# A hybrid block on one core: streamed projection weights prepared in the first stage, and the first gate folded into the output weight

## The chip, the cores and the metric

The kernel runs on one core of one Trainium2 chip. The metric is the device time of one execution in microseconds. Engines are named as in the profile: PE is TensorE (PEld its weight loads), DVE VectorE, ACT ScalarE, POOL GpSimd, SP SyncE, whose queue issues the DMAs. PE's clock is given as the granted clock, 1.00 being 2.4 GHz and 0.50 being 1.2 GHz.

## The reference

One layer over 2048 latent tokens and 256 context tokens of width 1024. `modulate` takes a shift and a scale from a matrix product with `mod_w`; one input projection feeds three mixers (gated linear attention, RWKV-7, retention), whose outputs are concatenated, projected, gated and added; a squared-ReLU MLP follows.

```python
def trunk_layer(xl, xc, c, c_ctx, p, rows, ctx_out):
    ml = jnp.split((jax.nn.silu(c) @ p["mod_w"] + p["mod_b"])[:, None, :], 6, axis=-1)
    ...
    zl = modulate(rms_norm(xl, p["norm1_g"]), ml[0], ml[1]) @ p["w_in"]
    zc = modulate(rms_norm(xc, p["norm1_g"]), mc[0], mc[1]) @ p["w_in"]
    ...
    xl = xl + ml[2] * (jnp.concatenate([yl_gla, yl_rwkv, yl_ret], axis=-1) @ p["w_out"])
    hl = modulate(rms_norm(xl, p["norm2_g"]), ml[3], ml[4])
    xl = xl + ml[5] * squared_relu_mlp(hl, p["mlp_w1"], p["mlp_w2"])
```

The output is a last RMS norm of the latent tokens. `ml[2]` is the first gate (g1 in the kernel).

## The kernel before

**Stages.** The first stage computes the modulation (`modulation1`), the normalised tokens as two float16 halves in SBUF (`h_block`: hT_hi, hT_lo), and the first part of the input projection. The scan then runs the chunks of the RWKV recurrence, the other mixers and the rest of the projection together. `out_proj` is the output projection with the second norm, `mlp` the rest.

**Projection in the first stage.** Columns of `w_in` are taken 128 at a time: L, G, k0, v0, r0, then k1, v1, r1, then k2, v2, r2 and three columns of the gated attention (called ga, gb, gc here). For each, `ip_tile` calls `ip_weights`: load (st), absmax by DVE (L343), the maximum over partitions by POOL (L345), two small DVE operations, a scaled float16 copy wh by ACT (L349) and the remainder wl by DVE (L350). `ip_block` (L390) does one block of 512 tokens, or 256 context tokens, with 24 matmuls (wh with hT_hi, wl with hT_hi, wh with hT_lo, eight each), evicts it on ACT with the scale (L393) and stores it (zc). In the code, the features of head group 0 (`rw_inputs`, `rw_features`: steps of many small operations on all engines, kk at L670 one of them) and `rw_base` (L794, L795) stand between r0 and k1; after r1 come `modulation2` and the first steps of group 1's features, and then k2 to gc. `modulation2` makes the other four rows of the modulation, 32 columns: a load mw, eight DVE operations (L269, L271), and a matmul with ones into one column of the PSUM tile pc (L272), which a second pool with one buffer holds; then mc, pg and the gate row.

**Order.** The instructions of an engine run in a fixed order. The framework sets it when the kernel is built, from the code's order, the priorities and the time at which buffers come free by its own estimate; a tile in a pool of one buffer can't be written before the one that held the buffer has been read. In the scan a planner (`Order`) picks which of its streams (chains of chunks, features, mixers, `ip_stream`) issues next, by estimated PE time; `ip_stream` is added with a count of 363 steps.

**The streamed projection.** `ip_stream` goes through five groups of two or three columns (`STREAM_T`; TV, two gate groups, two of retention), 14 columns in all. For each group it prepares the columns by `ip_weights` into rwh and rwl (one buffer each), then for each of 16 or 18 token tiles loads the stored normalised tokens (rh<-hd), runs 24 matmuls (L1027 is the line of all PE work in the scan), evicts (rzs, L443) and stores z (zt).

**The chains.** Four chunks make a block of the recurrence. Each chunk makes one ACT copy Tsf (L920).

**out_proj.** w_out is split in two float32r parts woh and wol (L1936). Each product pz (L1950) is multiplied by the gate row on DVE (gz, L1954) and added to x on POOL (L1955). Then the second norm: x times its factor (DVE, L1911), plus the shift row b2 (POOL, L1912), and sums of blocks as float16 halves (L1804, L1917, L1918).

Of the kernel before, what the change touches and what calls it, by code (L numbers as in the profile page):

```python
# [11 lines left out]
F32 = mybir.dt.float32  # L12
# [10 lines left out]
P = 128  # L23
# [54 lines left out]
def setup(k):  # L78
    nc, tc, I = k.nc, k.tc, k.I
    cp = k.cpool  # L80
    k.ones_row = cp.tile([1, P], F32, name="ones_row")
    nc.vector.memset(k.ones_row, 1.0)
# [69 lines left out]
def modulation1(k, xp, pp, then):  # L152
# [8 lines left out]
    with tc.tile_pool(name="mo1", bufs=1, side="right") as m1, tc.tile_pool(name="mo2", bufs=1, side="right") as mp:  # L161
# [16 lines left out]
        ones = mp.tile([P, P], F32, name="mones")  # L178
# [73 lines left out]
def modulation2(k, cp, first):  # L252
# [6 lines left out]
    with tc.tile_pool(name="mo2", bufs=2, side="right") as mp, tc.tile_pool(name="mops2", bufs=1, space=PSUM, side="right") as pp:  # L259
        ones = mp.tile([P, 1], F32, tag="ones", name="ones", bufs=1)  # L260
        nc.vector.memset(ones, 1.0)
        pc = pp.tile([P, 4 * KD], F32, tag="pc", name="pc", bufs=1)
# [19 lines left out]
        pt = pp.tile([4 * KD, P], F32, tag="pc", name="pg", bufs=1)  # L282
# [50 lines left out]
def ip_weights(k, wp, wh, wl, srcs, M):  # L333
# [8 lines left out]
    am = wp.tile([P, 1], F32, tag="am", name="am")  # L342
# [11 lines left out]
def ip_tile(k, nm, wp):  # L354
# [4 lines left out]
    return wh, wl, ip_weights(k, wp, wh[:, :, 0:M], wl[:, :, 0:M], srcs, M)  # L359


def ip_channels(k, names, wp, ps, ready=()):

    n = max(len(ready), 1)
    for group in [names[:n]] + [[nm] for nm in names[n:]]:
        tiles = ready if ready and group == names[:n] else [ip_tile(k, nm, wp) for nm in group]
# [5 lines left out]
        for bi in TOK_ORDER:  # L372
            for nm, *t in work:
                ip_block(k, nm, bi, wp, ps, *t)

# [36 lines left out]
def ip_stream(k, wp, ps):  # L412
# [3 lines left out]
    for cols in STREAM_T:  # L416
        W, kind = P * len(cols), cols[0][2]
        wh = wp.tile([P, KD, 384], F16, tag="rwh", name="rwh")
        wl = wp.tile([P, KD, 384], F16, tag="rwl", name="rwl")
        iv = []  # L420
        for u, (src, dst, _) in enumerate(cols):
            cs = slice(P * u, P * u + P)
            ar = ip_weights(k, wp, wh[:, :, cs], wl[:, :, cs], [(0, src, P)], P)
            iv.append(wp.tile([P, 2], F32, tag="iv", name="iv", bufs=6))
            nc.vector.tensor_scalar(iv[u], k.h_inv, ar, 48 ** -0.5 if kind == "v" else 1.0, ALU.mult, ALU.mult)
            yield 4
        yield 6
        for ti in range(2 if kind == "g" else 0, NT):
            n = 256 if ti < 2 and kind == "r" else W
            h = wp.tile([P, 2, KD, P], F16, tag="rh", name="rh", bufs=2)  # L430
# [11 lines left out]
            for u in range(n // P):  # L442
                nc.scalar.activation(zs[:, P * u : P * u + P], pz[:, P * u : P * u + P], AF.Copy, scale=iv[u][:, s : s + 1])  # L443
# [8 lines left out]
        k.streamed += 1  # L452

# [902 lines left out]
def mix_setup(k, mp, ps):  # L1356
# [5 lines left out]
    nc.tensor.matmul(pl, k.ones_row, rate, start=True, stop=True)  # L1362
# [445 lines left out]
def over_partitions(k, ps, pool, x):  # L1808
# [6 lines left out]
    nc.tensor.matmul(pt[:, P : P + 1], k.ones_row, m, start=True, stop=True)  # L1815
# [64 lines left out]
def out_proj(k, es, H, hp):  # L1880
# [6 lines left out]
    with tc.tile_pool(name="opy", bufs=2) as yp, tc.tile_pool(name="opx", bufs=2) as xp, tc.tile_pool(name="opps", bufs=4, space=PSUM) as ps:  # L1887
# [335 lines left out]
```

## Time and profile before

| | |
|---|---|
| timed, median of 3 | 3925.78 us (3912.99 to 3928.82) |
| the profiled execution | 3896.32 us |
| its span | 3894.5 us |
| PE busy | 3370.4 us, 87% |
| DVE busy | 2535.2 us, 65% |
| ACT, POOL busy | 1357.3 us, 35%; 786.4 us, 20% |
| mean granted clock | 0.887 |

The profile gives times from the start of the span. By it, the first stage lasts to about 640 us, the scan to about 2215, out_proj from 2240 to about 2480, and the MLP to the end.

### The profile page before, as it was taken

Reading aid. Unit: us, or ns where it says so; the run is one execution under the profiler, and the core shown is the slowest. Engines: PE = TensorE matmul, PEld = TensorE weight load, DVE = VectorE, ACT = ScalarE, POOL = GpSimd, SP = SyncE. Lnnn points to the kernel's source line nnn. Section 1 sums busy time; section 2 is a strip of 40 time slices with the busy share of each in tenths; the row PEclk is TensorE's granted clock in tenths of the full one; section 3 lists DMA queues with packets and bytes.
Section 4 is the critical chain, followed back from the end, with each engine's and each line's share of the span. In section 5 each row is a group of like instructions: output and inputs, shape, how many; then the busy total and the mean of one; then the engine's idle time right before and its main releaser. Section 6 shows DMA issues by size and latency. Waiting matters only on the chain. (4 is left out here: it accounts for less than half of the span.)

```text
span 3894.5 us, 62894 instructions
## 1 busy us (share of the span) xinstructions
PE 3370.4 (87%) x23493; PEld 2263.0 (58%) x23493; DVE 2535.2 (65%) x5307; ACT 1357.3 (35%) x3033; POOL 786.4 (20%) x940
## 2 busy tenths in 40 slices
PE   7687786699798789899899688888899999999997
PEld 2443445476466567666676566555555566666665
DVE  7555877567585666757567368877777766544446
ACT  3333343334344443525344333333333332221212
POOL 3122335214343122222232235200000001000001
PEclk8898895698788789789898799999999999999998
DMA  7875646345454244343423276653333346322322
GB/s 228 191 210 147 185 143 175 109 137 158 124 165 116 85 113 114 98 102 110 121 88 111 66 211 195 231 186 124 125 128 127 130 123 207 114 90 97 104 87 95
DMA packets 526339, 532.36 MB, mean 137 GB/s; under 512 B 247171, under 2 KB 408710, under 8 KB 525254
## 3 DMA queue, kind: packets, MB, share of 16 engines
q1 hardware_dynamic: 526024, 528.25, 45.6%
q8 instruction: 187, 3.06, 0.3%
q14 instruction: 128, 1.05, 0.1%
HBM read 323.81 MB, written 180.19 MB: 129 GB/s over the span
## 5 line engine op out<-in xcount | busy, mean ns | idle before, releaser
L2005 PE MATMUL pu<-H,wo 128*128 128x512 f16 x2688 | 625.5, 387 | 27.6 <-ACT wo L1841 21.1
L2071 DVE TENSOR_TENSOR acc<-acc,pz 128x512 f32<-128x512 f32 x512 | 348.3, 685 | 373.0 <-PE pz L2069 370.0
L2005 PEld LDWEIGHTS <-wo 128*128 128x128 f16 x2688 | 254.3, 99 | 361.8 <-issue 63.9
L2069 PE MATMUL pz<-w2h,uh 128*128 128x512 f32 x1024 | 439.5, 429 | 27.3 <-ACT uh L2032 25.1
L2069 PE MATMUL pz<-w2l,uh 128*128 128x512 f32 x1024 | 409.7, 400 | 0.0
L2069 PE MATMUL pz<-w2h,ul 128*128 128x512 f32 x1024 | 396.7, 396 | 1.0 <-DVE ul L2034 1.0
L2084 POOL TENSOR_TENSOR acc<-acc,fg 128x1024 f32<-128x1024 f32 x10 | 23.9, 2411 | 1368.7 <-ACT acc L2083 1368.7
L1027 PE MATMUL pz<-rwh,rh 128*128 128x384 f16 (+1 forms) x1376 | 289.0, 340 | 7.7 <-ACT rzs L443 4.8
L1027 PEld LDWEIGHTS <-rh 128*128 128x128 f16 x2064 | 199.5, 105 | 132.5 <-issue 37.9
L2069 PEld LDWEIGHTS pz<-w2h,uh 128*128 128x128 f32 x1024 | 199.0, 194 | 84.4 <-ACT uh L2032 27.4
L2069 PEld LDWEIGHTS pz<-w2l,uh 128*128 128x128 f32 x1024 | 198.8, 194 | 41.2
L2069 PEld LDWEIGHTS pz<-w2h,ul 128*128 128x128 f32 x1024 | 195.4, 191 | 44.6 <-DVE ul L2034 1.4
L390 PEld LDWEIGHTS <-wh 128*128 128x128 f16 (+2 forms) x1072 | 115.8, 111 | 171.9 <-issue 73.1
L2029 ACT ACTIVATE u<-u 128x512 f32<-128x512 f32 x64 | 36.8, 622 | 484.4 <-DVE s L2023 484.4
L390 PE MATMUL pz<-hT_hi,wh 128*128 128x512 f16 (+5 forms) x536 | 133.7, 392 | 61.9 <-ACT zs L393 50.7
L2017 ACT ACTIVATE s<-pu,iv 128x512 f32<-128x512 f32 x96 | 65.5, 685 | 255.9 <-PE pu L2005 255.6
L1027 PE MATMUL pz<-rwl,rh 128*128 128x384 f16 (+1 forms) x688 | 146.0, 344 | 0.7 <-DVE rwl L350 0.7
L1027 PE MATMUL pg<-Z,BK 64*128 64x128 f32 (+1 forms) x864 | 127.3, 320 | 8.4 <-DVE fbon L986 4.9
L1950 PE MATMUL pz<-woh,yh 128*128 128x512 f32 x256 | 104.8, 415 | 26.5 <-DMA x<-in_w_out_dram 16.0
L390 PE MATMUL pz<-hT_lo,wh 128*128 128x512 f16 (+5 forms) x536 | 127.0, 377 | 0.0
L390 PE MATMUL pz<-hT_hi,wl 128*128 128x512 f16 (+5 forms) x536 | 125.2, 374 | 0.0
L1027 PEld LDWEIGHTS pg<-Z,BK 64*128 64x128 f32 x864 | 107.6, 218 | 21.1 <-issue 6.2
(524 smaller groups left out, 7043.0 us busy)
## 6 DMA issues: line engine op xcount, KB each, us to landing
rh<-hd SPq DMA_DIRECT2D x86, 512.0 KB
st<-in_mlp_w_dram SPq DMA_DIRECT2D x64, 512.0 KB
w1d<-wo SPq DMA_DIRECT2D x112, 256.0 KB
wo<-w1d SPq DMA_DIRECT2D x112, 256.0 KB
x<-in_x_dram SPq DMA_DIRECT2D x32, 512.0 KB
mw<-in_mod_w_dram SPq DMA_DIRECT2D x32, 512.0 KB
w2d<-w2h SPq DMA_DIRECT2D x32, 512.0 KB
w2d<-w2l SPq DMA_DIRECT2D x32, 512.0 KB
```

The lines of the kernel that those rows point to most:

```text
L390: nc.tensor.matmul(pz[:M, o : o + step], a[:, kk, 0:M], b[:, kk, t0 + o : t0 + o + step], start=(i == 0), stop=(i == 23))
L1027: return op(out, lhs, rhs, **kw)
L1950: nc.tensor.matmul(pz, a[:, kk], w[:, kk, 512 * hf : 512 * hf + 512], start=(kk + i == 0), stop=(kk == KD - 1 and i == 2))
L2005: nc.tensor.matmul(bank, W[o][:, a, kk], H[o][:, 4 * b + kk], start=(i == 0), stop=(i == 11))
L2017: nc.scalar.activation(s, product(o), AF.Copy, scale=iv)
L2029: nc.scalar.activation(r, r, AF.Relu)
L2069: nc.tensor.matmul(pz, U[q][tb][u][:, ts], W2[q][w][:, cs], start=(i == 0), stop=(i == 5))
L2071: nc.vector.tensor_add(a[:, cs], a[:, cs], pz)
L2084: nc.gpsimd.tensor_mul(a, a, fg)
```

## The change

1. `ip_weights` takes its scale from the sum of squares of the column tile in place of the largest absolute value: ACT squares with an accumulated sum, a matmul with ones (pnrm) adds over partitions, and five small DVE operations make the scale (`norm_scale`). The matmul writes a bank of a new PSUM pool `ipn` with one buffer; modulation2's pc and pg now use that pool and its one buffer too.
2. `ip_channels` prepares the next column ahead of the present one's blocks, and calls `ip_keep` twice after each column behind the first group. `ip_keep` prepares one streamed column and stores both halves to DRAM (wsd), and keeps its scales in SBUF (siv). The 14 calls fall to k1 to ga.
3. `ip_stream` reads a group's weights back with one DMA for each half; the high half of the next group is loaded one token tile ahead. The tag rw has three buffers for both halves. The planner's count is 345.
4. `out_proj` multiplies the rows of w_out by g1 on DVE before they are split; pz is added to x straight on DVE; b2 is added on DVE.
5. The ones tile lives on; two smaller tiles of ones are gone.

```diff
+def norm_scale(k, ps, pool, sq):
+    nc.tensor.matmul(ps, k.ones, sq, start=True, stop=True)
+    x = pool.tile([P, 1], F32, tag="ar", name="ar", bufs=6)
+    nc.vector.tensor_scalar(x, ps, 1e-36, None, ALU.max)
...
+    nc.vector.tensor_scalar(si, x.bitcast(I32), 1, None, ALU.logical_shift_right)
+    nc.vector.tensor_scalar(si, si, -1, 0x5F3759DF, ALU.mult, ALU.add)
+    nc.vector.tensor_scalar(s, s, 0.96 * 2.0 ** 14, None, ALU.mult)
+    nc.vector.reciprocal(x, s)
+    return s, x
...
-    nc.vector.tensor_reduce(am, st[:, :, 0:M], axis=AX.XY, op=ALU.max, apply_absolute_value=True)
-    ar = wp.tile([P, 1], F32, tag="ar", name="ar", bufs=6)
-    nc.gpsimd.partition_all_reduce(ar, am, P, bass_isa.ReduceOp.absmax)
-    nc.vector.tensor_scalar(ar, ar, 1e-30, 2.0 ** -14, ALU.max, ALU.mult)
-    sc = wp.tile([P, 1], F32, tag="sc", name="sc")
-    nc.vector.reciprocal(sc, ar)
+    sq = wp.tile([P, 1], F32, tag="am", name="am")
+    nc.scalar.activation(wh, st[:, :, 0:M], AF.Square, accum_out=sq)
+    sc, ar = norm_scale(k, ps, wp, sq)
     nc.scalar.activation(wh, st[:, :, 0:M], AF.Copy, scale=sc)
     nc.vector.scalar_tensor_tensor(wl, st[:, :, 0:M], sc, wh, ALU.mult, ALU.subtract)
...
+def ip_keep(k, wp):
...
+    g, u = k.keep.pop(0)
+    src, _, kind = STREAM_T[g][u]
+    w = [wp.tile([P, KD, P], F16, tag="w" + x, name="kw" + x, bufs=3) for x in "hl"]
+    ar = ip_weights(k, wp, k.ipn.tile([P, 512], F32, tag="pn", name="pnrm")[:, 0:1], *w, [(0, src, P)], P)
+    k.nc.vector.tensor_scalar(k.siv[:, g, u], k.h_inv, ar, 48 ** -0.5 if kind == "v" else 1.0, ALU.mult, ALU.mult)
+    for d, x in zip(k.wsd[g], w):
+        k.nc.sync.dma_start(d[:, :, P * u : P * u + P], x)
...
     n = max(len(ready), 1)
-    for group in [names[:n]] + [[nm] for nm in names[n:]]:
-        tiles = ready if ready and group == names[:n] else [ip_tile(k, nm, wp) for nm in group]
+    groups = [names[:n]] + [[nm] for nm in names[n:]]
+    tiles = list(ready) or [ip_tile(k, names[0], wp, k.ipn)]
+    for i, group in enumerate(groups):
...
+        ahead = following() if len(group) == 1 else None
...
+        for _ in range(2 if n == 1 else 0):
+            ip_keep(k, wp)
+        tiles = following() if ahead is None else ahead
...
-    with tc.tile_pool(name="mo2", bufs=2, side="right") as mp, tc.tile_pool(name="mops2", bufs=1, space=PSUM, side="right") as pp:
-        ones = mp.tile([P, 1], F32, tag="ones", name="ones", bufs=1)
-        nc.vector.memset(ones, 1.0)
-        pc = pp.tile([P, 4 * KD], F32, tag="pc", name="pc", bufs=1)
+    with tc.tile_pool(name="mo2", bufs=2, side="right") as mp:
+        pp, ones = k.ipn, k.ones[:, 0:1]
+        pc = pp.tile([P, 512], F32, tag="pn", name="pc")[:, 0 : 4 * KD]
...
-        pt = pp.tile([4 * KD, P], F32, tag="pc", name="pg", bufs=1)
+        pt = pp.tile([P, 512], F32, tag="pn", name="pg")[0 : 4 * KD, 0:P]
...
+    def weights(g, i):
+        w = wp.tile([P, KD, 384], F16, tag="rw", name="rw" + "hl"[i], bufs=3)
+        nc.sync.dma_start(w[:, :, 0 : P * len(STREAM_T[g])], k.wsd[g][i])
+        return w
+
+    wh = weights(0, 0)
+    for g, cols in enumerate(STREAM_T):
         W, kind = P * len(cols), cols[0][2]
-        wh = wp.tile([P, KD, 384], F16, tag="rwh", name="rwh")
-        wl = wp.tile([P, KD, 384], F16, tag="rwl", name="rwl")
-        iv = []
-        for u, (src, dst, _) in enumerate(cols):
-            cs = slice(P * u, P * u + P)
-            ar = ip_weights(k, wp, wh[:, :, cs], wl[:, :, cs], [(0, src, P)], P)
-            iv.append(wp.tile([P, 2], F32, tag="iv", name="iv", bufs=6))
-            nc.vector.tensor_scalar(iv[u], k.h_inv, ar, 48 ** -0.5 if kind == "v" else 1.0, ALU.mult, ALU.mult)
-            yield 4
-        yield 6
+        wl = weights(g, 1)
+        if g == 0:
+            yield 8
         for ti in range(2 if kind == "g" else 0, NT):
             n = 256 if ti < 2 and kind == "r" else W
+            if ti == NT - 1:
+                nxt = weights(g + 1, 0) if g + 1 < len(STREAM_T) else None
...
-                nc.gpsimd.tensor_add(x, x, b2)
+                nc.vector.tensor_add(x, x, b2)
...
+            g1 = mod_row(k, xp, 0)
...
+                nc.vector.tensor_mul(st, st, g1)
                 nc.scalar.copy(wh[:, kk], st)
                 nc.vector.tensor_tensor(wl[:, kk], st, wh[:, kk].bitcast(F32), ALU.subtract)
-            with tc.issue_after(load):
-                g1 = mod_row(k, xp, 0)
...
-                        gz = xp.tile([P, 512], F32, tag="gz", name="gz")
-                        nc.vector.tensor_mul(gz, pz, g1[:, cs])
-                        nc.gpsimd.tensor_add(x[:, cs], x[:, cs], gz)
+                        nc.vector.tensor_add(x[:, cs], x[:, cs], pz)
...
+            k.ipn = es.enter_context(tc.tile_pool(name="ipn", bufs=1, space=PSUM, side="right"))
             ip_channels(k, names, wp, ips, ready)
...
-            k.order.add(ip_stream(k, fp, fps), 0, 312, 363, 4)
+            k.order.add(ip_stream(k, fp, fps), 0, 312, 345, 4)
```

**PE in the first stage.** Before, in the midst of the columns k1 to gc, PE's rows are these (L390 the blocks, pc the modulation's columns):

```order
L390 MATMUL pz<-hT_hi,wh 128x256
L272 MATMUL pc<-ones,macc 128x1
L390 LDWEIGHTS wh
L390 MATMUL pz<-hT_hi,wh 128x256
L390 LDWEIGHTS wh
L390 MATMUL pz<-hT_hi,wh 128x256
L390 LDWEIGHTS wh
L390 MATMUL pz<-hT_hi,wh 128x256
L272 MATMUL pc<-ones,macc 128x1
```
The pc matmuls and the features' matmuls lie between the matmuls of the blocks, no more than eight rows of the printed order apart, to the end of the projection. In the changed kernel (L421 is the block, L269 pc, L334 pnrm; pv, pk, pb, px, pu and pn belong to a feature step) PE comes to the end of r1's last block with these rows:

```order
L421 MATMUL pz<-hT_lo,wh 128x512
L421 LDWEIGHTS wh
L421 MATMUL pz<-hT_lo,wh 128x512
L334 MATMUL pnrm<-am,ones 128x1
L682 MATMUL pv<-ident,v 128x128 x3
L334 MATMUL pnrm<-am,ones 128x1
L269 MATMUL pc<-ones,macc 128x1 x2
L784 MATMUL pk<-ident,knw 128x128 x3
L682 MATMUL pv<-ident,E 128x128 x3
L714 MATMUL pb<-s,bones 128x384
L741 MATMUL px<-AR,BK 64x64 x24
L661 MATMUL pu<-LS,w_1503 128x384
```
Some 80 rows of this kind follow, with po for rw_base, until the last pc column and pg, and behind them k2's first matmuls:

```order
L682 MATMUL pv<-ident,v 128x128 x3
L269 MATMUL pc<-ones,macc 128x1
L280 MATMUL pg<-ident,mc_3662 32x128
L839 MATMUL po<-ident,Yin 64x72 x8
L334 MATMUL pnrm<-am,ones 128x1
L784 MATMUL pk<-ident,knw 128x128 x3
L682 MATMUL pv<-ident,E 128x128 x3
L334 MATMUL pnrm<-am,ones 128x1
L421 LDWEIGHTS wh
```
Between the last block of r1 and the first of k2 stand all 32 pc matmuls and seven feature steps (a pn each), which lay among the blocks before. The 28 blocks of k2 to gc follow with a few feature matmuls among them, and the scan's first chunk behind those.

**SP at the start of the second streamed group.** Before (st is a column's weights, L431 a tile of tokens, AR, BK and bon the features' stores):

```order
L341 DMA st<-in_w_in_dram 128x8x128 [waits DMAHW1_49,DVE_49]
L726 DMA BK_91<-BK 64x6x64 [waits DMAHW2_49,DVE_49]
L723 DMA AR_86<-AR 128x768 [waits DVE_49,DMAHW3_49,Activation_49,Pool_49]
L726 DMA BK_92<-BK 64x6x64 [waits DMAHW4_49,DVE_49]
L724 DMA BK_91<-BK 64x768 [waits DMAHW5_49,Pool_49]
L725 DMA BK_91<-BK 64x6x64 [waits DMAHW6_49]
L724 DMA BK_92<-BK 64x768 [waits DMAHW7_49,Pool_49]
L725 DMA BK_92<-BK 64x6x64 [waits DMAHW0_49]
L682 DMA bon_107<-s 128x384 [waits DMAHW1_49,DVE_49]
L341 DMA st<-in_w_in_dram 128x8x128 [waits DMAHW2_49,DVE_49]
```
In the changed kernel, from the row where the second group's low half is read back (ws1l):

```order
L450 DMA rwl<-ws1l 128x3072 [waits DMAHW4_49,PE_49]
L758 DMA BK_102<-BK 64x768 [waits DMAHW5_49,Pool_49]
L759 DMA BK_102<-BK 64x6x64 [waits DMAHW6_49]
L758 DMA BK_103<-BK 64x768 [waits DMAHW7_49,Pool_49]
L759 DMA BK_103<-BK 64x6x64 [waits DMAHW0_49]
L716 DMA bon_118<-s 128x384 [waits DMAHW1_49,DVE_49]
L483 DMA zt<-rzs 128x384 [waits DMAHW2_49,Activation_49]
L464 DMA rh<-hd 128x2048 [waits DMAHW3_49,PE_49]
L450 DMA rwh<-ws2h 128x3072 [waits DMAHW4_49]
```
Where three column loads, each waiting for DVE's use of an st buffer, lay apart, one load waits for PE's last use of the buffer, and the next group's high half follows eight rows behind.

**DVE in out_proj.** Before, around the first second-norm operations (the 128x1024 rows of x):

```order
L1911 SCALAR_TENSOR_TENSOR x_31058<-x_31058,rsy,mrow 128x1024 [waits DMAHW4_49,DMAHW0_49,DVE_49]
L1954 TENSOR_TENSOR gz<-pz,mrow 128x512 [waits PE_49,Pool_49]
L1911 SCALAR_TENSOR_TENSOR x_31060<-x_31060,rsy,mrow 128x1024 [waits DMAHW5_49,Pool_49]
L1918 SCALAR_TENSOR_TENSOR hl<-x_31058,h_s_3500,hl 128x512 [waits Activation_49]
L1954 TENSOR_TENSOR gz<-pz,mrow 128x512 [waits PE_49]
L1804 TENSOR_TENSOR xsum<-x_31060 128x512 [waits Pool_49]
L1804 TENSOR_TENSOR xsum<-x_31058,x_31060 128x512
```
and in the changed kernel:

```order
L1945 SCALAR_TENSOR_TENSOR x_31237<-x_31237,rsy,mrow 128x1024 [waits DMAHW7_49,DMAHW6_49,DVE_49]
L1946 TENSOR_TENSOR x_31237<-x_31237,mrow 128x1024 [waits DMAHW5_49,DVE_49]
L1945 SCALAR_TENSOR_TENSOR x_31239<-x_31239,rsy,mrow 128x1024 [waits DMAHW1_49]
L1952 SCALAR_TENSOR_TENSOR hl<-x_31237,h_s_3664,hl 128x512 [waits Activation_49]
L1987 TENSOR_TENSOR x_31418<-x_31418,pz 128x512 [waits DMAHW0_49,PE_49]
L1946 TENSOR_TENSOR x_31239<-x_31239,mrow 128x1024 [waits DVE_49]
L1932 TENSOR_TENSOR yst<-yst,yh 128x1024 [waits DMAHW2_49,Activation_49]
```
gz, the product with the gate row, is now the addition to x itself (L1987), and a 128x1024 addition (L1946) stands behind each L1945; POOL's L1955 and L1912 have no counterpart there.

## Rows read from the trace of the kernel before

**Rows 1.** The page's first line:
```profile
span 3894.5 us, 62894 instructions
```
**Rows 2.** Windows: length, busy us (count) PE, PEld, DVE, ACT, POOL; clock, DMA share, GB/s:
```profile
960.00:1040.00 80.00, 52.11 (x469) 35.46 (x468) 41.58 (x106) 23.23 (x66) 24.48 (x26) 0.66 0.38 111
1240.00:1320.00 80.00, 53.47 (x511) 38.76 (x510) 48.55 (x116) 41.54 (x90) 20.68 (x34) 0.72 0.44 106
1320.00:1580.00 260.00, 237.55 (x2450) 172.65 (x2450) 169.17 (x420) 115.03 (x296) 70.23 (x93) 0.88 0.41 111
1580.00:1660.00 80.00, 63.63 (x589) 48.32 (x587) 59.01 (x161) 36.03 (x78) 13.47 (x24) 0.67 0.33 85
1910.00:1980.00 70.00, 54.01 (x696) 42.57 (x696) 46.32 (x127) 31.49 (x95) 19.74 (x25) 0.76 0.30 89
2240.00:2480.00 240.00, 211.89 (x855) 159.68 (x855) 189.04 (x272) 86.22 (x118) 100.39 (x51) 0.93 0.67 202
```
**Rows 3.** Tile Tsf by window: count, duration ns min/median/max, first and last start:
```profile
L920 ACT COPY Tsf<-ptf x5: 212/212/212, 650.9 to 771.8; 128x64 f32<-128x64 f32 x5
...
L920 ACT COPY Tsf<-ptf x9: 212/213/232, 771.8 to 858.5; 128x64 f32<-128x64 f32 x9
...
L920 ACT COPY Tsf<-ptf x5: 193/218/220, 953.6 to 1039.3; 128x64 f32<-128x64 f32 x5
...
L920 ACT COPY Tsf<-ptf x5: 212/212/224, 1246.0 to 1320.6; 128x64 f32<-128x64 f32 x5
...
L920 ACT COPY Tsf<-ptf x21: 193/212/270, 1320.6 to 1580.1; 128x64 f32<-128x64 f32 x21
...
L920 ACT COPY Tsf<-ptf x5: 212/212/226, 1580.1 to 1656.2; 128x64 f32<-128x64 f32 x5
...
L920 ACT COPY Tsf<-ptf x5: 212/212/222, 1924.5 to 1974.6; 128x64 f32<-128x64 f32 x5
```
**Rows 4.** Second group's start: POOL's timeline, ACT's line L349, one window:
```profile
981.87 0.41 POOL L345 PARTITION_ALL_REDUCE ar<-am  x1 [5.92 <-issue]
...
L349 ACT ACTIVATE rwh<-st,sc x14: 1132/1148/1176, 681.9 to 1938.9; 128x1024 f16<-128x1024 f32 x14
...
980.00:990.00 10.00, 0.12 (x5) 0.00 (x0) 2.19 (x5) 1.31 (x2) 1.45 (x3) 0.58 0.24 72
```
**Rows 5.** PE's timeline in a projection block: start, us, line, names, count:
```profile
154.51 1.89 PE L390 MATMUL pz<-hT_hi,wh 128*96 128x512 f16 x8
...
159.69 1.89 PE L390 MATMUL pz<-hT_hi,wh 128*112 128x512 f16 x8
```
**Rows 6.** DVE and its releasers, 330 to 650: window, kk, lines, POOL's wait:
```profile
341.00:646.00 305.00, 242.13 (x577) 0.82 0.58 164
...
L670 DVE SCALAR_TENSOR_TENSOR kk<-k,par,pk x9: 601/608/615, 340.9 to 646.5; 128x384 f32<-128x384 f32 x9
...
L271 DVE SCALAR_TENSOR_TENSOR macc<-mw,cs,macc 128x128 f32<-128x128 f32 x175 | 66.1, 405 | 1.0
L794 DVE TENSOR_TENSOR xtmp<-Xin,Lin 72x4 f32<-72x4 f32 (+14 forms) x30 | 17.0, 566 | 0.2
L635 DVE TENSOR_TENSOR_SCAN c<-seg,c 128x384 f32<-128x384 f32 x16 | 16.0, 998 | 22.2 <-POOL c L633 22.2
L795 DVE TENSOR_REDUCE Xin<-xtmp 72x4 f32<-72x4 f32 (+14 forms) x30 | 14.7, 490 | 0.3
...
POOL c L633 <- issue: 21.9, 3, 7.6
```
**Rows 7.** DMA, 140 to 180 us: packets, and the queue's share of 16 engines:
```profile
DMA packets 21157, 6.98 MB, mean 175 GB/s; under 512 B 19953, under 2 KB 20468, under 8 KB 21155
...
q1 hardware_dynamic: 21155, 6.96, 79.8%
```
**Rows 8.** out_proj: lines (ns min/median/max), and DVE's timeline at 2305 and 2306:
```profile
L1955 POOL TENSOR_TENSOR x<-x,gz x32: 1262/1693/2589, 2267.6 to 2470.4; 128x512 f32<-128x512 f32 x32
...
L1912 POOL TENSOR_TENSOR x<-x,mrow x16: 2344/3108/3381, 2282.4 to 2491.1; 128x1024 f32<-128x1024 f32 x16
...
L1954 DVE TENSOR_TENSOR gz<-pz,mrow x32: 677/683/693, 2266.7 to 2469.7; 128x512 f32<-128x512 f32 x32
...
2305.65 0.16 DVE L147 TENSOR_TENSOR rst<-rst,rsh 128x2 f32<-128x2 f32 x1
...
2306.71 1.15 DVE L147 TENSOR_TENSOR rst<-rst,rsh 128x2 f32<-128x2 f32 x1
...
L1861 DVE TENSOR_TENSOR st<-st,mrow x32: 1202/1224/1228, 2475.2 to 3155.1; 128x1024 f32<-128x1024 f32 x32
```

More of the change, by code (lines that the diff above doesn't have):

```diff
@@ L80, in setup @@
     cp = k.cpool
-    k.ones_row = cp.tile([1, P], F32, name="ones_row")
-    nc.vector.memset(k.ones_row, 1.0)
     k.bones = cp.tile([P, P], F32, name="bones")
@@ L177, in modulation1 @@
         nc.sync.dma_start(g, I["norm1_g"].to_broadcast([P, D]))
-        ones = mp.tile([P, P], F32, name="mones")
+        ones = k.ones = cp.tile([P, P], F32, name="ones")
         nc.gpsimd.memset(ones, 1.0)
@@ L330, in h_block, with ip_weights @@
         k.turned.append(nc.sync.dma_start(k.hl[:, :, c], lo, transpose=True).ins)
-def ip_weights(k, wp, wh, wl, srcs, M):
+def norm_scale(k, ps, pool, sq):
+    nc = k.nc
+    nc.tensor.matmul(ps, k.ones, sq, start=True, stop=True)
+    x = pool.tile([P, 1], F32, tag="ar", name="ar", bufs=6)
+    nc.vector.tensor_scalar(x, ps, 1e-36, None, ALU.max)
+    s = pool.tile([P, 1], F32, tag="sc", name="sc", bufs=2)
+    si = s.bitcast(I32)
+    nc.vector.tensor_scalar(si, x.bitcast(I32), 1, None, ALU.logical_shift_right)
[3 more added lines that the diff above has]
+    return s, x
+def ip_weights(k, wp, ps, wh, wl, srcs, M):
     nc = k.nc
@@ L351, in ip_weights, with ip_tile @@
     return ar
-def ip_tile(k, nm, wp):
+def ip_tile(k, nm, wp, ps, tag="pn"):
     srcs, M, _ = CT[nm]
@@ L358, in ip_tile, with following @@
     wl = wp.tile([P, KD, P], F16, tag="wl", name="wl", bufs=3)
-    return wh, wl, ip_weights(k, wp, wh[:, :, 0:M], wl[:, :, 0:M], srcs, M)
+    return wh, wl, ip_weights(k, wp, ps.tile([P, 512], F32, tag=tag, name="pnrm")[:, 0:1], wh[:, :, 0:M], wl[:, :, 0:M], srcs, M)
+def ip_keep(k, wp):
+    if not k.keep:
+        return
+    g, u = k.keep.pop(0)
[5 more added lines that the diff above has]
+        k.nc.sync.dma_start(d[:, :, P * u : P * u + P], x)
 def ip_channels(k, names, wp, ps, ready=()):
     n = max(len(ready), 1)
-    for group in [names[:n]] + [[nm] for nm in names[n:]]:
-        tiles = ready if ready and group == names[:n] else [ip_tile(k, nm, wp) for nm in group]
+    groups = [names[:n]] + [[nm] for nm in names[n:]]
+    tiles = list(ready) or [ip_tile(k, names[0], wp, k.ipn)]
+    for i, group in enumerate(groups):
+        def following():
+            return [ip_tile(k, nm, wp, k.ipn) for nm in groups[i + 1]] if i + 1 < len(groups) else []
+        ahead = following() if len(group) == 1 else None
         work = []
@@ L442, in ip_stream @@
             for u in range(n // P):
[L443 removed]
+                nc.scalar.activation(zs[:, P * u : P * u + P], pz[:, P * u : P * u + P], AF.Copy, scale=k.siv[:, g, u, s : s + 1])
             z = zs[:, 0:n]
@@ L452, in ip_stream @@
         k.streamed += 1
+        wh = nxt
 NCH = T // 64
@@ L1361, in mix_setup @@
     pl = ps.tile([P, 8], F32, tag="mx", name="pl")
-    nc.tensor.matmul(pl, k.ones_row, rate, start=True, stop=True)
+    nc.tensor.matmul(pl, k.ones[0:1], rate, start=True, stop=True)
     k.rlg = mp.tile([P, 2, 4], F32, name="rlg")
@@ L1814, in over_partitions @@
     nc.vector.tensor_reduce(m, pt[0:1, 0:P], axis=AX.X, op=ALU.max)
-    nc.tensor.matmul(pt[:, P : P + 1], k.ones_row, m, start=True, stop=True)
+    nc.tensor.matmul(pt[:, P : P + 1], k.ones[0:1], m, start=True, stop=True)
     return pt[:, P : P + 1]
@@ L2113, in tile_hybrid_block @@
     k.hd = dp.tile([NT, P, 2, KD, P], F16, name="hd")
+    k.wsd = [[dp.tile([P, KD, P * len(cols)], F16, name=f"ws{g}{x}") for x in "hl"] for g, cols in enumerate(STREAM_T)]
+    k.keep = [(g, u) for g, cols in enumerate(STREAM_T) for u in range(len(cols))]
+    k.siv = cp.tile([P, len(STREAM_T), 3, 2], F32, name="siv")
     rw_dram(k, dp)
@@ L2128, in tile_hybrid_block @@
                 ready = []
-                first, rest = modulation1(k, xp, mps, lambda: ready.append(ip_tile(k, names[0], wp)))
+                first, rest = modulation1(k, xp, mps, lambda: ready.append(ip_tile(k, names[0], wp, mps, "pb")))
                 hp, lp = (es.enter_context(tc.tile_pool(name="hT" + i, bufs=1, side="right")) for i in "hl")
```

6 lines of the change are left out of this document (2 added, 4 removed).

## The prediction

> **What bounds the kernel now.** I read the stage windows first, then the start times of the scan's blocks, then the weight preparation inside the scan, then DVE in the first stage, and out_proj last. The span is 3894.5 us [rows 1]; from about 2500 us to the end the MLP runs, which the diff doesn't touch, so the change plays in the first 2500 us.
>
> In the scan PE sets the pace: in 1320 to 1580 it is busy 237.55 of 260 us at a granted clock of 0.88. In four stretches it isn't: 52.11 of 80 us at 0.66 (960 to 1040), 53.47 of 80 at 0.72, 63.63 of 80 at 0.67, 54.01 of 70 at 0.76 [rows 2]. These lie where the stream goes to its next group of columns. The chains tell the same: four chunks (five Tsf copies, first to fifth) take 51.9 us on the mean from 1320.6 to 1580.1, but 85.7, 74.6, 76.1 and 50.1 us across the four group starts [rows 3]. There each column of weights is loaded, reduced on DVE, reduced over partitions on POOL (0.41 us behind 5.9 us in which POOL waits for nothing that the trace shows), scaled on ACT (1.15 us) and subtracted on DVE, one column after the other; from 980 to 990 PE is busy 0.12 us [rows 4].
>
> In the first stage PE and DVE share the bound: from 341 to 646 PE does projection blocks between the features' small matmuls, and DVE is busy 242 of 305 us, a share of 0.79 [rows 6]. A projection block of 512 tokens takes 5.18 us at full clock (three runs of eight matmuls, 154.51 to 159.69) [rows 5].
>
> **1. Scan, what is removed.** The 14 preparations leave; the 10 read-back loads come. What the four later group starts cost I get in two ways. By the blocks: 85.7 + 74.6 + 76.1 + 50.1 less four times 51.9 is 79 us [rows 3]. By PE's work (busy time times clock): the four stretches, 310 us long, did 34.4 + 38.5 + 42.6 + 41.0 = 156.5 us of it; at the 0.80 per us of 1320 to 1580 that takes 195 us, so 115 are lost [rows 2]. The second holds the half clock that outlasts a start, the first doesn't; I take the middle, 97. What comes in its place: the high halves load one tile ahead, but the low half of a group (768 KB) goes into a buffer that the last group's last matmuls free, so it starts when PE is done with them and SP holds everything behind it till then (the order of SP shows BK and bon stores, a zt store and an rh load there). PE has the high-half matmuls of one tile and some chain work to run meanwhile. No row shows this load. From below it is hidden (0); from above it goes at the 175 GB/s of the busiest small-packet stretch [rows 7], 4.5 us, with as much again of queue: 9. I take 3 for each of four starts, 12, near the lower end since the DMA share there is 0.30 to 0.44 [rows 2]. **Scan: -85** (-115 to -45).
>
> **2. First stage, what the order turns over.** The sums of squares go through a matmul into a PSUM pool of one bank (ipn), and modulation2's pc now lives in the same bank. pc collects 32 one-column matmuls, each behind eight DVE operations, and is held until pg has been read; k2's norm waits for that. So in PE's order all 32 pc matmuls, seven feature steps and rw_base(0) stand between the last block of r1 and the first of k2, where before the blocks lay between them; then 28 blocks follow nearly bare, and only then the scan. DVE's work decides when k2 starts:
> - DVE's 256 modulation operations cost 0.40 us each, 102 us; 200 of them came after 340 before (the 175 shown and the 25 first ones of a column) [rows 6], so 56 (22 us) leave ahead of the second step's kk at 340.9. It comes at about 319, the third at 345 (a step and kept columns between).
> - From there to k2: 102 us of modulation, 31.7 of rw_base(0) (L794 with L795, 17.0 and 14.7), and seven feature steps. A step: 242 less 75 (modulation), 31.7 and about 8 (two preparations) leaves 127 over eight steps, 15.9; seven make 111. Sum 245; with step prices from the whole trace I get 265. I take 255.
> - DVE's share: 0.79 as before if every wait stays. Of its 63 idle us 22.2 were waits for POOL's c, which itself sat 21.9 us without a cause shown, three times [rows 6]; three all-reduces stood on POOL there, and one is left. Without two thirds of this, and without PE's blocks in the way, I take 0.88: 290 us, so k2 starts at 635. Bounds: 245 at 0.95 gives 603, 265 at 0.79 gives 680.
> - 28 blocks, 24 of them of 512 and four of 256 tokens, are 26 times 5.18, 135 us [rows 5]; 143 with a start at half clock (138 to 153). From the first chunk to the fifth: the next eight took 86.7 us [rows 3] for 7.5 stream tiles and 478 other matmuls; the order has some 4 and 359 here, so 60 (58 to 65).
> - 635 + 143 + 60 = 838, against 771.8 for the fifth chunk before [rows 3]. From there the streams, features and chains left to do are equal within two tiles. **Hand-over: +66** (+27 to +126).
>
> The rest of the first stage: 28 Squares on ACT (1.15 us each, the shape of rwh [rows 4]) and five DVE operations of a few elements (0.16 us for such a one [rows 8]) take the place of an absmax and the POOL chain of 6 us; ACT isn't late there. 28 stores of 256 KB and the 14 loads, which only move, are new in this stage; on SP each store waits there for its column's halves, with the z stores and the features' loads behind it, for the two or three us of a preparation whose loads are prefetched. For a column of k2 to ga 3.7 MB are moved (three loads, four stores, z) in the 23.3 us of its blocks; the stretch 140 to 180, with 19,953 of 21,157 packets under 512 B, moved 175 GB/s at a share of 0.80 [rows 7], so 17 us: hidden, 0 (0 to +10).
>
> A rule speaks against these stores. The Trainium skill, "DMA: Bandwidth & Descriptors", section Specifications, wants 512 B for line rate and says that below it the engine does a read-modify-write; the stores go in 256 B pieces. If that doubled their 1 MB a column, an estimate by that page, the 17 us become 22, still under 23.3, and the sum stays; the row shows small packets at near the mean rate, so I give the rule little of rival C.
>
> **3. out_proj.** Added on DVE: eight rows of w_out times g1, 1.22 us each as in L1861, 9.8 us; b2's 16 additions, moved from POOL (3.1 us there), 19.5 us at the same 1.22; 2.6 for g1, which now loads ahead. The 32 gz multiplications (0.68) become 32 additions from PSUM of the same shape. Off the path: POOL's 32 additions (1.69 us) and its 16 [rows 8]. What comes back: while POOL works, DVE's operations with two SBUF inputs are stretched: the same L147 takes 0.16 us, and 1.15 at 2306.71 [rows 8]. I sum the excess over each group's fastest to 45 us of DVE's 189 in this stage [rows 2], gz with its PSUM input nearly none. 40 of it return: -8 (-20 to +5), since DVE is busy 189 of 240 and PE 212, neither alone the bound [rows 2].
>
> The rule that bears on this: the Trainium skill, "SBUF — State Buffer", section Who interferes with whom, says that a VectorE operation with two SBUF inputs shares its second read path with GpSimd as an exclusive lock, and one with a single SBUF input doesn't. L147 and gz agree. By it all 45 return, -13 in place of -8.
>
> **Sum:** 66 - 85 - 8 = -27 us on the profiled run. That run (3896 us) lies 29.5 below the median of the timed runs, 3925.8, so I take the change to the median: 3899.
>
> **The rivals.**
> - **B, slower: the one bank.** Mechanism: pc holds the only bank, k2's norm waits, and PE's 135 us of blocks come behind DVE's work and no longer beside it. If DVE keeps its 0.79 with 265 us of work, the hand-over costs 126; with 70 from the scan and 8 from out_proj that is +48, 3974. For: DVE's waits for POOL and loads stood there with PE free as well. Against: fewer POOL reductions. It decides from a hand-over of 93 on, the fifth chunk later than 865.
> - **C, the wait is only exchanged.** The low halves come late, and with SP held also the rh loads behind them: 12 us at each start, 48 in place of 12, or the small stores hold the loads of k2 to ga. -27 + 36 = +9, 3935. Against: DMA's share there.
> - **D, more.** DVE at 0.95 with 245 us: +27; the scan gives 105, out_proj 12: -90, 3836. For: 0.95 needs only that the modulation fills DVE's gaps.
> - That it doesn't do what it says: the planner's stream count falls from 363 to 345, so tiles could bunch; the order shows 41 tiles at the middle chunk before, 49 after, and 80 of 86 in both near the end. I put it into C.
>
> **How the numbers follow.** A measurement of this kernel can tell about 0.5%, 20 us. Forecast 0.52, its own range -60 to +8: 0.36 of it faster, 0.16 same. B 0.20: 0.17 slower, 0.03 same. C 0.12: 0.08 same, 0.04 slower. D 0.16: faster. Faster 0.52, same 0.27, slower 0.21. Both signs hold much of it: the forecast alone is 3866 to 3934; 8 in 10 reaches over half of D and most of B: 3850 to 3975.
>
> **What would show it.** In the profile of the changed kernel: (1) no PE window in the scan under 8 of 10 us at a group start; four chunks across one in 50 to 58 us, else step 1 is wrong. (2) The first block of k2 near 635, PE nearly idle at half clock for 200 us ahead of it, and the fifth chunk near 838; if k2 starts well before 600, the bank doesn't hold it back. (3) DVE's share from 345 to k2 near 0.88. (4) PE's waits for rwl: 12 us in all. (5) out_proj 8 shorter, L147 at 0.16 all through. It is wrong above all if the hand-over differs: 0.1 of DVE's share is some 30 us.

## The result

Over 20 runs of each, the changed kernel takes 3877.5 us (median) and the kernel before 3918.1: ratio 0.9893, 95% interval 0.9874 to 0.9912, by the ratio 42 us less. A second comparison gave 0.9917 (0.9892 to 0.9943), 32 us less. The ratios leave out runs in the slower of two states, and gains in us are taken from the ratios and not from the medians. The forecast was faster, 27 us less, 3899 us. The direction and the range held; the gain came out half as large again, and inside the sum all three terms were off, by 49, 23 and 18 us, partly against each other. Of the 22 us by which the forecast time was too high, 8 are the base (the three runs of before that it started from had a median of 3925.8, twenty have 3918.1) and 14 the gain.

The profiled execution of the changed kernel took 3890.3 us, 13 above its median run; that of before, 3896.3, lay 22 below its own. The two traces alone would show 6 us. Each run lists its mean granted clock, and it differs between the profiles: 0.878 in this one, 0.887 in that of before. Over all runs (30 of the changed kernel, 40 of before) a kernel's time falls by about 3 us for 0.001 of clock. So below, where a stage is compared, several traces with the same order of instructions stand for each kernel, not one pair.

**The first stage after.** Windows of the changed kernel (columns as in [rows 2]), from the end of r1's last block to k2's first, then k2 to gc, then up to the fifth chunk:

```profile
331.00:578.00 247.00, 100.27 (x703) 80.84 (x701) 222.36 (x568) 88.19 (x219) 96.58 (x124) 0.53 0.58 161
578.00:728.00 150.00, 144.66 (x756) 72.97 (x757) 46.26 (x115) 52.75 (x85) 11.09 (x12) 0.97 0.57 166
728.00:816.00 88.00, 79.50 (x794) 56.75 (x792) 62.71 (x152) 33.77 (x105) 37.45 (x46) 0.77 0.65 177
```

For 247 us PE is busy 100 us, at half clock, while DVE is busy 222; then the 28 blocks run nearly bare at full clock with DVE busy 46 of 150. The two engines work one after the other. PE's longest wait in the first of these stretches, and DVE's lines there:

```profile
PE pc L269 <- DVE macc L268: 42.4, 14, 7.5
```
```profile
L268 DVE SCALAR_TENSOR_TENSOR macc<-mw,cs,macc 128x128 f32<-128x128 f32 x206 | 80.9, 407 | 0.5
...
L669 DVE TENSOR_TENSOR_SCAN c<-seg,c 128x384 f32<-128x384 f32 x14 | 13.5, 967 | 0.7 <-POOL c L667 0.7
```

The wait for POOL's c, 22.2 us in [rows 6], is 0.7: with all but one of the reductions over partitions gone from POOL there, its long pauses ahead of c are gone too.

**The chains after.** The first four chunks, two stretches of four with a group's read-back at 966 and 1207 us, and one without (Tsf as in [rows 3]):

```profile
L954 ACT COPY Tsf<-ptf x5: 212/212/220, 744.3 to 816.0; 128x64 f32<-128x64 f32 x5
...
L954 ACT COPY Tsf<-ptf x5: 192/212/212, 945.8 to 991.8; 128x64 f32<-128x64 f32 x5
...
L954 ACT COPY Tsf<-ptf x5: 209/212/213, 1150.4 to 1213.4; 128x64 f32<-128x64 f32 x5
...
L954 ACT COPY Tsf<-ptf x5: 193/212/219, 1250.7 to 1321.8; 128x64 f32<-128x64 f32 x5
```

46.0 and 63.0 us across the read-backs, where [rows 3] has 85.7 and 74.6 across the starts. But the last row, 71.1 us without a read-back in it, is of the same four chunks as the 74.6 of before: these are long for more than the group's start. And the chain from the fifth chunk to the last takes 1344.5 us against 1382.8, 38 less and not 85.

### The profile page after: what moved, and what is told of

Same layout as the page of the kernel before. It is cut to its first block, busy times and chain, and to the rows that moved or that the text cites. A ratio compares the mean times of both kernels' runs of the same rounds, so it can differ in the third digit from the quotient of the medians.

```text
span 3888.5 us, 63001 instructions
## 1 busy us (share of the span) xinstructions
PE 3406.2 (88%) x23549; PEld 2314.3 (60%) x23549; DVE 2511.2 (65%) x5385; ACT 1392.3 (36%) x3089; POOL 675.8 (17%) x864
## 5 line engine op out<-in xcount | busy, mean ns | idle before, releaser
L2101 PE MATMUL pz<-w2h,uh 128*128 128x512 f32 x1024 | 442.3, 432 | 26.4 <-ACT uh L2064 23.7
L421 PEld LDWEIGHTS <-wh 128*128 128x128 f16 (+2 forms) x1072 | 113.9, 109 | 149.4 <-issue 34.4
L421 PE MATMUL pz<-hT_hi,wh 128*128 128x512 f16 (+5 forms) x536 | 125.5, 378 | 45.7 <-ACT zs L424 24.9
L1061 PE MATMUL pg<-Z,BK 64*128 64x128 f32 (+1 forms) x864 | 144.4, 343 | 5.6 <-issue 1.6
L1061 PEld LDWEIGHTS pg<-Z,BK 64*128 64x128 f32 x864 | 121.0, 237 | 20.3 <-issue 6.9
L1984 PE MATMUL pz<-woh,yh 128*128 128x512 f32 x256 | 99.9, 403 | 30.3 <-DMA x<-in_w_out_dram 21.6
L421 PE MATMUL pz<-hT_hi,wl 128*128 128x512 f16 (+5 forms) x536 | 121.2, 370 | 0.0
L421 PE MATMUL pz<-hT_lo,wh 128*128 128x512 f16 (+5 forms) x536 | 120.2, 367 | 0.0
```

The source lines that it names most:

```text
L421: nc.tensor.matmul(pz[:M, o : o + step], a[:, kk, 0:M], b[:, kk, t0 + o : t0 + o + step], start=(i == 0), stop=(i == 23))
L1061: return op(out, lhs, rhs, **kw)
L1984: nc.tensor.matmul(pz, a[:, kk], w[:, kk, 512 * hf : 512 * hf + 512], start=(kk + i == 0), stop=(kk == KD - 1 and i == 2))
L2101: nc.tensor.matmul(pz, U[q][tb][u][:, ts], W2[q][w][:, cs], start=(i == 0), stop=(i == 5))
```

## The experiments

All ratios are against the kernel before, in runs of the same chip.

**The parts: out_proj alone, and the rest alone.** The first is the kernel before with the out_proj edits of the diff and nothing else, the second the changed kernel without them.

> The kernel before with the out_proj edits alone (g1 folded into the rows of w_out, the addition from PSUM on DVE, b2 on DVE). PE's order is that of before up to out_proj. The prediction's third step: -8 us, 0.998 of before (bounds -20 to +5). From the two traces: product start to product end 225.0 before and 214.4 after, to the end of the span 4.5 less, so -10 to -15, 0.996 to 0.9975. Rival, DVE becomes the bound in out_proj and the gain is given back in the MLP's start: 1.000.

Measured: 0.9958 (0.9935 to 0.9981), -16 us.

> The changed kernel with out_proj as before, so steps 1 and 2 alone; PE's order is that of the changed kernel up to out_proj. If the parts add up: before times 0.9893 plus what out_proj gave, 0.991 to 0.993 of before (-26 to -33 us). Its profile is a second look at the changed first stage and scan: by the prediction's terms the fifth chunk of the first chain late by 44 to 66 and the scan from there shorter by 85; if the scan's gain is only the 35 us of the one trace there is, this trace shows 25 to 45 again, and steps 1 and 2 together nothing (1.000).

Measured: 0.9984 (0.9954 to 1.0014), -6 us. So steps 1 and 2, most of the change, can't be told from nothing here; what is clear of noise is out_proj. Its trace repeats the hand-over: the fifth chunk at 822.0, with before's order at 771.8 and 775.8. From there to the last chunk it takes 1326.6 us, 56 less than before, more than the 25 to 45 expected from one trace and less than the forecast's 85.

**The changed kernel again.**

> The changed kernel once more, on the chip of the two runs below, with a second profile. Its time against before was 0.9893; out_proj alone gave 0.9958 and steps 1 and 2 alone 0.9984, together 0.994. If those add up, this run comes out at 0.991 to 0.995; if the parts help each other, at 0.988 to 0.990. Its trace: fifth chunk at 812 to 826 (816 and 822 in the two traces with this first stage), PE's idle time in the scan 90 to 100 us, and half-clock time with PE busy between 340 and 400 (379 and 346 there, 312 and 303 with the scan of before).

Measured: 0.9917 (0.9892 to 0.9943); with it the parts add up (0.994) within their intervals, while the first comparison's 0.9893 lies at the edge of what they allow. The fifth chunk came at 814.4, PE's idle time in the scan was 91 us, and its busy time at half clock 408, above the 340 to 400 expected.

**The bank.**

```diff
-    with tc.tile_pool(name="mo2", bufs=2, side="right") as mp:
-        pp, ones = k.ipn, k.ones[:, 0:1]
-        pc = pp.tile([P, 512], F32, tag="pn", name="pc")[:, 0 : 4 * KD]
+    with tc.tile_pool(name="mo2", bufs=2, side="right") as mp, tc.tile_pool(name="mops2", bufs=1, space=PSUM, side="right") as pp:
+        ones = k.ones[:, 0:1]
+        pc = pp.tile([P, 512], F32, tag="pc", name="pc")[:, 0 : 4 * KD]
...
-            with ... tc.tile_pool(name="rbaps", bufs=2, space=PSUM) as bps:
+            with ... tc.tile_pool(name="rbaps", bufs=1, space=PSUM) as bps:
```

> The changed kernel with modulation2's pc and pg in a bank of their own again (rw_base's PSUM pool gives up one of its two banks). In PE's order the blocks of k2 to gc then lie among the pc matmuls and the feature steps, as before. If the one bank costs what the trace shows, the fifth chunk comes at 765 to 785 in place of 816, and the kernel gains 30 to 50 us on the changed one: 0.977 to 0.982 of before. Rival: the features go slower with blocks among them (kk of the tenth step at 646.5 before, 576.9 in the changed kernel) and the gain is under 15 us: 0.986 to 0.990.

Measured: 3767 us, 0.9655 (0.9621 to 0.9690): 135 us faster than before and 93 faster than the change as made (0.9893), about twice the most that was expected. The same 247 us as above, and the first four chunks, in its trace:

```profile
331.00:578.00 247.00, 199.20 (x1264) 114.70 (x1265) 210.15 (x570) 117.42 (x257) 87.01 (x104) 0.89 0.77 214
```
```profile
L954 ACT COPY Tsf<-ptf x5: 201/213/218, 641.2 to 706.7; 128x64 f32<-128x64 f32 x5
```

PE is now busy 199 of the 247 us at 0.89, and DVE still 210: side by side. The fifth chunk comes at 706.7, 109 earlier than in the changed kernel; from there to the last chunk the two take the same (1340 and 1341 us, the second a mean of three traces). Out_proj's first product starts 73 us behind the last chunk, in the changed kernel's traces 98 to 108; but in the second kernel with a bank of its own (more stores, below) it is 96, so this part isn't shown to be the bank's. That kernel repeats the first part: the fifth chunk at 696.8.

**Absolute maxima back, and so no use of the bank by the weights.**

```diff
-    sq = wp.tile([P, 1], F32, tag="am", name="am")
-    nc.scalar.activation(wh, st[:, :, 0:M], AF.Square, accum_out=sq)
-    sc, ar = norm_scale(k, ps, wp, sq)
...
+    nc.vector.tensor_reduce(am, st[:, :, 0:M], axis=AX.XY, op=ALU.max, apply_absolute_value=True)
...
+    nc.gpsimd.partition_all_reduce(ar, am, P, bass_isa.ReduceOp.absmax)
+    nc.vector.tensor_scalar(ar, ar, 1e-30, 2.0 ** -14, ALU.max, ALU.mult)
...
+    nc.vector.reciprocal(sc, ar)
```

> The changed kernel with the scales by absolute maxima as before (DVE reduction, POOL over partitions), so that no weight tile needs the one bank and modulation2 has it alone; all else as in the change. In PE's order the blocks of k2 to gc lie among the pc matmuls again. If the bank is what costs 110 us (own bank 0.9655, changed kernel 0.9893), this comes to 0.966 to 0.975: the bank's price back, less what POOL's reductions cost in the first stage (kk of the first step at 270 with sums of squares, 298 before). Rival, that the own bank's gain came from the smaller pool of rw_base or another order by chance: 0.98 or more.

Measured: 3843 us, 0.9847 (0.9805 to 0.9888): the blocks lie among the pc matmuls again, and it is a little faster than the change as made, but not 0.966 to 0.975; it lies where the rival was expected (0.98 or more), so the time alone doesn't decide between the bank and the rival. DVE's waits in its trace, 331 to 740:

```profile
DVE ar L359 <- POOL ar L358: 46.0, 13, 6.8
DVE c L673 <- POOL c L671: 21.6, 6, 7.3
```

With 14 more preparations in the first stage, POOL's reductions hold DVE for 46 us and, through c, for 22 more; the fifth chunk comes at 828.5, as late as with the bank, and 122 later than with sums of squares and a bank of its own. 68 of the 122 are these waits, which the kernel with its own bank hasn't (none for ar, under 2 us for c); the rest isn't traced. So the sums of squares are worth much, and the one bank took that back: two effects of about 100 us each at the fifth chunk, which the forecast had seen only as their difference. For the bank, and against the rival, speaks PE's busy time from 331 to 578: 164 us at 0.79 here, with rw_base's pool as in the change, 199 and, in the second such kernel, 189 with a bank of its own, 100 in the changed kernel. What rw_base's smaller pool does alone was not run. That this kernel is faster than the change as made, though its fifth chunk comes as late, lies further on in its one trace: 1312 us from there to the last chunk, with PE busy at half clock for 257 us of them (378 on the mean of the changed order's three traces), and 64 to the first product. Why, isn't shown.

**What the preparation in the scan cost.**

```diff
+        if cols is STREAM_T[0]:
+            wh = wp.tile([P, KD, 384], F16, tag="rwh", name="rwh")
+            wl = wp.tile([P, KD, 384], F16, tag="rwl", name="rwl")
+            iv = []
-        for u, (src, dst, _) in enumerate(cols):
+        for u, (src, dst, _) in enumerate(cols if cols is STREAM_T[0] else ()):
```

> The kernel before without the preparation of the streamed weights behind the first group: groups two to five use the first group's weights and scales. What the four later group starts cost in all, in the kernel before. The prediction's 97 us (79 to 115): 0.970 to 0.980 of before, with no block of four chunks over 65 us. Rival: what the starts lose is idle time of PE (63 us less idle in the changed kernel's trace over the scan) that the half clock then gives back, as in the changed kernel's trace, where the scan is shorter by 35: 0.988 to 0.992.

Measured: 0.9874 (0.9843 to 0.9906), -49 us: half of 97, and at the rival's end. Not all blocks are under 65 us: the four chunks from 1279.7 to 1359.2 take 79.5, without any preparation. The scan, fifth chunk to last, of before, of this kernel, and of the changed one, each in one window:

```profile
772.00:2155.00 1383.00, 1222.64 (x13286) 898.11 (x13285) 918.30 (x2475) 576.51 (x1619) 404.81 (x566) 0.86 0.42 117
```
```profile
768.00:2099.00 1331.00, 1242.61 (x13309) 912.97 (x13308) 898.60 (x2419) 570.23 (x1613) 401.24 (x561) 0.87 0.43 118
```
```profile
816.00:2161.00 1345.00, 1247.96 (x13150) 924.68 (x13146) 882.86 (x2383) 560.12 (x1588) 387.91 (x546) 0.85 0.42 117
```

PE's idle time (length less busy) goes from 160 to 88 and 97 us. The clock stays: 0.86, 0.87, 0.85. PE's busy time grows by 20 to 25 us for nearly the same matmuls. In the changed kernel this is the half clock: its three traces have PE busy at half clock for 346 to 408 us of this stretch, the four with before's order for 303 to 355. In the kernel without preparation it is 324, the mean of before's order, and why its busy time grows isn't shown. What a removed stall gave is its idle time less this growth; the half clock of the four stretches in [rows 2] did not go with the stalls.

**The read-back.** The eight later loads are left out: `wl = weights(g, 1)` only for the first group, `nxt = wh`.

> The changed kernel without the read-back of the weights behind the first group (groups two to five use the first group's): what the eight loads still cost. The prediction took 12 us (0 to 36): 0.986 of before where the changed kernel has 0.9893. If the loads are hidden, as PE's waits in the trace say, the same as the changed kernel within 0.3%.

Measured: 0.9898 (0.9857 to 0.9940), beside 0.9917 for the changed kernel on the same chip: 7 us, well inside the intervals; no cost is shown. In the changed kernel's trace nothing on PE waits for rwl: the load at 966.4 is followed, to 1000, by a longest PE wait of 1.6 us, and the one lull behind a load (PE busy 4.24 us from 1885 to 1895, the load at 1877.6) is mostly a wait of 4.1 us for an ACT operation of another mixer (rkd). The next high half is issued 6 us behind the load at 966.4, a whole group ahead.

**The two halves of out_proj.** First the fold of g1 with the addition from PSUM, b2 on POOL; then b2 on DVE alone.

> The kernel before with the first half of the out_proj edits: g1 folded into the rows of w_out and the addition from PSUM on DVE; b2 stays on POOL. Both edits together gave 0.9958 (-17 us), where the prediction had -8. By the prediction's prices the fold adds 12 us to DVE and takes POOL's 32 additions away (52 us of POOL, most of what stretches DVE's operations): 0.9965 to 0.9985. If the gain is the contention between POOL and DVE, most of it is here; if it is the chain (x waits for POOL's b2, ACT's hl for that), most is in the other half and this is 0.999 to 1.001.

> The kernel before with b2's additions on DVE in place of POOL, the other half. By the prediction's prices alone: 19.5 us more on DVE, POOL's 3.1 us of each off the chain from x to hl: 0.998 to 1.001. If the chain is the gain: 0.996 to 0.998.

Measured: the fold 1.0007 (0.9986 to 1.0027), b2 on DVE 0.9966 (0.9945 to 0.9987), -13 us. By these times nearly the whole gain of out_proj is the step that the forecast had as a cost of 19.5 us. The traces say more. From the first product to about the last, before, with the fold, with b2 on DVE, and with both:

```profile
2244.00:2461.00 217.00, 198.52 (x803) 154.24 (x803) 172.18 (x247) 72.83 (x100) 96.30 (x49) 0.94 0.66 193
```
```profile
2263.00:2471.00 208.00, 193.09 (x796) 151.53 (x796) 159.39 (x255) 74.27 (x104) 45.36 (x19) 0.96 0.69 196
```
```profile
2261.00:2472.00 211.00, 196.03 (x805) 152.12 (x806) 175.25 (x264) 74.43 (x104) 59.08 (x36) 0.96 0.69 201
```
```profile
2246.00:2447.00 201.00, 194.18 (x815) 152.41 (x816) 164.38 (x276) 76.94 (x108) 7.45 (x5) 0.97 0.71 208
```

Each half shortens the products, by 9 and 6 us, and both by 16; PE's idle time there goes from 18 to 15, 15 and 7 us. With the fold alone this is lost again at the start of the MLP, where PE waits for DVE's maxima of its weights (1.3 us in the trace of before):

```profile
PE pmx L1812 <- DVE am L1830: 21.9, 1, 21.9
```

Its first product of w2h comes 40.6 us behind out_proj's last, 26.4 before and 17.7 with both halves. The stretching of DVE beside POOL, summed as in the forecast (each group's excess over its fastest), falls from 43 us to 22, 29 and 7: 36 us less, close to the 40 that the forecast took, and moving b2 costs DVE 3 us of busy time and not 19.5. ACT's hl waits for b2's step as long as before (37.9 us with b2 alone on DVE, 32.3 with POOL), at 1.22 us each there and 3.1 on POOL [rows 8]; so the shorter step in the chain isn't shown to be the gain. How much is the stretching and how much POOL's pace isn't separated.

**More stores.** To the kernel with its own bank, every kept half stored a second time.

> The kernel with modulation2's bank of its own, and each kept half stored twice, the second time to a DRAM tensor that nobody reads: 28 more stores of 256 KB in 256-byte pieces. By the prediction (the stores are hidden, 17 of 23 us a column with one store): the same as without, 0.962 to 0.970. By the rule that pieces under 512 bytes cost a second pass, one store already takes 22 of 23 us, and a second one makes the loads of k2 to ga late: 0.972 or more.

Measured: 3743 us, 0.9542 (0.9502 to 0.9582): faster, not slower. The extra stores move some instructions of the first stage, so this is no clean doubling; but it shows that 28 more stores in 256-byte pieces cost nothing that can be seen. It is 1.1% faster than the kernel without them, on another chip; that this is the order, moved by chance, is likely but not shown. In its trace, from 341 to 646:

```profile
DMA packets 122189, 71.10 MB, mean 233 GB/s; under 512 B 70044, under 2 KB 112628, under 8 KB 122162
```

More than half of the packets are under 512 B, and the rate is higher than the 175 GB/s of [rows 7]. The read-modify-write that the Trainium skill names for pieces under 512 B ("DMA: Bandwidth & Descriptors", Specifications) is not seen as time in any run here.

## Why the prediction was right or wrong

The table has the prediction's terms beside what several traces show: for the changed kernel those of the change, its repeat and the kernel without the out_proj edits; for before, that of before and the three with before's order (out_proj edits, whole and in halves). For out_proj they are the seven traces with both edits (1623.5 to 1630.2) and the three with neither (1650.4 to 1654.2).

| term | forecast | measured |
|---|---|---|
| fifth chunk, against before | +66 | 817.5 less 774.4: +43 |
| chain, fifth chunk to last | | 1341 less 1387: -46 |
| last chunk to first product | | 101 less 92: +10 |
| scan, the two rows above | -85 | -36 |
| out_proj, first product to the end | -8 | 1627 less 1653: -26; timed alone -16 |
| sum | -27 | -19; timed -42 and -32 |

In the first three rows, the three traces of the changed order are of executions 8 us above their kernels' medians on the mean (13, 6, 4), the four of before's order of executions 11 below (22, 23, 0, 0): with these 19 the sum is -38, between the two timed values. So step 1 gave 49 less than forecast, and steps 2 and 3 together 41 more; that the total was missed by no more than 15 us is luck.

**Step 1, the scan: failed.** The price of the group starts, "I take the middle, 97", is 49 us when measured alone. Both readings behind it charged the starts with what wasn't theirs. The second counted all half-clock time of the four stretches as lost to the starts; without the starts, the scan has as much half-clock time with PE busy (324 us, as on the mean with before's order). The first compared with the blocks beside a start as if they stayed as they were; without any start, four chunks take 51.7 us on the mean (1331 us for 103 chunks), where 79 us less would have needed 50.6, and one block still takes 79.5. Idle time was the part to count: 72 us less of it without the starts, 20 of these given back as longer busy time. In the changed kernel's three traces it is 65 us less idle, 19 given back, and 10 lost behind the last chunk, where the forecast had no term: 36 in place of 85. The read-back's 12 us are neither shown nor excluded by the runs; PE doesn't wait for it in the trace.

**Step 2, the hand-over: right in its mechanism, short in its sizes.** pc held the bank, PE's order did what the rows of the order say, PE sat at half clock for 247 us. k2's first block came at 578, not 635, below the lower bound of 603: DVE's work there was 222 us, not 255 (92 of the modulation's 102 were left, and a step costs about 14 us, not 15.9), the second step's kk came at 301, not 319, and DVE's share was 0.90 for 0.88. Of the two reasons given for the share, POOL's pauses are seen to go (22.2 to 0.7); how much of the share is theirs and how much PE's blocks being away isn't separated (with the blocks back, in the kernel with its own bank, it is 0.85). The blocks took 150 us for 143 and the first four chunks with what lay ahead of them 88 for 60. These errors go both ways, and the step gave 23 us more than forecast. What it didn't see is that +43 is the difference of two large numbers: without the shared bank the change brings the fifth chunk to 707, 68 earlier than before, and the bank costs 111. Rival B named the mechanism; its price was taken against the kernel before, where it should have been taken against the change without it.

**Step 3, out_proj: right in what returns, wrong in what it is worth.** DVE got 36 us of stretching back where the forecast had 40, but the term is 16 timed and 26 in the traces, not 8. The forecast set the returned time against 32 us of DVE work added and counted the balance; PE's waits, which it didn't count, fell by some 12 us between the products, and the start of the MLP, which it left out, came earlier with both edits and later with the fold alone. "b2's 16 additions [...] 19.5 us" was a price that nothing paid: moving them alone gains 13 us.

**Rivals.** C's loads and stores are not seen: without the read-back the time is the same within 19 us either way, and PE is busy 144.66 of 150 us in k2 to gc. Of D, k2 came at 578, earlier than the 603 of its 0.95, with less work at a share of 0.90, but the scan gave much less than D needed. That the stream would bunch can't be told apart from the other moves of the order.

## What to carry to other kernels

A buffer that is shared by a long accumulation and by a short step in another loop puts the loops one behind the other, in an order fixed at build time; look in the order of the changed kernel for what stands between two neighbours of before, and price it against the change without the sharing, since giving the accumulation a bank of its own turned 1% into 3.5%. A stall's price here was its idle time, less what the rest then ran longer, and not the half clock around it. A cost on the busier engine isn't yet a cost of the kernel: the step that looked like 20 us more on DVE was a gain, and half of an edit can lose at the next stage what it gains in its own.

## What the runs showed of the hardware

The half clock (0.50, 1.2 GHz) can last long with PE busy all the time. In the changed kernel, two windows:

```profile
1945.00:1953.00 8.00, 7.01 (x101) 5.73 (x98) 6.99 (x19) 3.90 (x12) 3.80 (x6) 1.00 0.39 125
1956.00:2026.00 70.00, 70.00 (x504) 57.95 (x502) 24.74 (x70) 14.84 (x45) 11.31 (x14) 0.50 0.14 41
```

and PE's timeline where the clock fell:

```profile
1953.52 0.43 PE L1061 MATMUL rpy<-rV,rA 128*128 128x64 f32 x2 [1.51 <-DVE rA L1755]
```

There is one wait of 1.5 us, and the next 70 us, without a gap, run at half clock; the same work at full clock would take some 35 (an estimate, if its pace goes with the clock). That this wait set it off isn't shown. It is float32 matmuls of 32 to 128 columns for the most part. Where such stretches fall differs from trace to trace of one kernel (1985 to 2005 is at 0.50 in this trace and at 0.85 in its repeat), and the mean clock of a run goes with its time (3856 us at 0.885, 3901 at 0.873). The Trainium skill, "TensorE: Matmul & The Clock Gate", Part 1, says that the gate follows how busy PE has been of late; this trace, with PE busy 70.00 of 70 us at 0.50, doesn't agree if busy is what the profile counts. The runs don't show what decides how long the half clock stays.

POOL's reduction over partitions comes with more than itself: 5.9 us without a cause shown ahead of it [rows 4], and some 7 more ahead of the next c on POOL [rows 6], which DVE waits for (22.2 us before, 21.6 with absolute maxima in the changed kernel, 0.7 without). The runs show that the pauses go with the reductions, not what POOL does in them.
